# The first mixer's projection begins over half of the features, and the modulation pieces are dealt out differently

## The chip, the cores and the metric

One core of one Trainium2 chip runs the whole program as a single launch. A core has five engines that each take their instructions strictly in the order in which they were queued: TensorE (PE, with its weight load PEld), VectorE (DVE), ScalarE (ACT), GpSimd (POOL) and SyncE (SP, which here only issues DMA transfers). The metric is the device time of one execution in microseconds (us), as the median of several.

## The reference, cut to what matters

Two layers of a transformer-like trunk over 512 latent tokens and 256 context tokens, 1024 features, fp32. The change touches the first mixer of layer 0 alone:

```python
mod_l = silu(c) @ mod_w[l] + mod_b[l]            # 6 x 1024 values: shift, scale, gate, twice
h = x * (1 + scale) + shift                      # the same for the context with c_ctx
z = h @ w_in                                     # 1024 -> 1536 features: 512 pool, 512 a, 512 gate
u = z_a * sigmoid(z_gate)                        # then a depthwise convolution over 31 tokens
y = silu(layer_norm(conv(u)))                    # 4 groups of 128 channels
p = mean over windows of 2, 4, 8, 16 tokens - z_pool, then a 128x128 product per group
out = concat(p, y) @ w_out
```

After it come a residual, a norm and the PEER retrieval, then layer 1 with another mixer. All matrix products of the mixer split each fp32 operand in a high and a low part and add three products.

## The kernel before, in words

**Modulation.** `mod_w` of both layers is cut in 24 pieces of 1024 x 512, 2 MB each; pieces 0 to 11 are layer 0's, and of these 0 and 1 are the first shift (features 0 to 511, and 512 to 1023), 2 and 3 the first scale. `mod_pieces` (L179) loads a piece into one of three buffers `modw`, multiplies it on PE (32 matmuls into `modp`, 64 records in the trace), and copies it on ACT into a row buffer `mrow` (four copies a piece). Its inner function `turned` transposes the row on PE (`modt`, L72 and L198) and adds the bias on DVE (L203, and L205 for a scale). `mods(...)` first turns the group begun before, then begins a new one, so a group is turned one `mods` later. `modp` and `modt` have one buffer each: a group's transposes wait until DVE has read the group before.

**Projection.** Pieces 0, 2, 1, 3 are worked first, then x is loaded in eight blocks of 128 features (`xt`, four buffers), modulated on DVE (L467) and split in `h1h` (ACT) and `h1l` (DVE). The projection then runs in twelve chunks of 128 output features. A chunk is 48 matmuls (8 feature blocks, 3 products, 512 and 256 tokens) into one of three PSUM buffers `zps`; its weights are loaded by SP (`c_raw`, two buffers) and split on ACT (`c_hi`) and DVE (`c_lo`) into three buffers. The first eight chunks come in four pairs (value and gate), then four pool chunks. After a pair, ACT computes the sigmoid `sg` (L545) and DVE the product `upad` (L547, L548).

**Convolution.** Group 0's 31 taps are done as a scaling on ACT (`ctap`, L500, two buffers) and an addition on POOL (`cacc`, L501); groups 1 and 2 as one DVE instruction a tap (L496); group 3 on PE as products with diagonal matrices (`cdh` on ACT L511, `cdl` on DVE L512, six buffers each; six matmuls a tap), which start after the last chunk. `advance(6)` after a chunk queues four taps of each group that runs.

**Pool and end.** `pooled` (L576) forms sums of windows on DVE (`psum`, L584), multiplies and splits them, and a small product on PE follows. The output weights (`wo_raw`, `woh`, `wol`) are split in the same stretch. When all taps are done, a mean over channels is taken on PE with `invn` (L617), and the norm follows.

**What sets the order.** The program is traced in the order written; a list scheduler with a time model of its own then fixes every engine's queue at compile time. At run time the queues are in-order and only semaphores hold an instruction back. After the mean with `invn` the order of PE, DVE and ACT is the same in both kernels to the end of the program, and SP's and POOL's too from before that point on.

Of the kernel before, what the change touches and what calls it, by code (L numbers as in the profile page):

```python
# [9 lines left out]
F32 = mybir.dt.float32  # L10
# [8 lines left out]
P = 128  # L19
D = 1024  # L20
KB = D // P
NLAT, NCTX = 4, 2
NTOK = (NLAT + NCTX) * P
# [52 lines left out]
def kernel(tc, a, out):  # L76
    nc = tc.nc
    V, S, G, PE, SP = nc.vector, nc.scalar, nc.gpsimd, Tracked(nc.tensor), nc.sync
# [7 lines left out]
    def pool(stack, name, bufs=1, space=None, side="left"):  # L86
        return stack.enter_context(tc.tile_pool(name=name, bufs=bufs, space=space, reuse_waits="tile") if space
                                   else tc.tile_pool(name=name, bufs=bufs, side=side, reuse_waits="tile"))
# [9 lines left out]
    def kt(shape, name, dt=F32):  # L98
        return kp.tile(shape, dt, name=name)
# [75 lines left out]
    mrow = [kt([P, P], f"mrow{i}") for i in range(2)]  # L175
# [2 lines left out]

    def mod_pieces(js, room, pp, queue, after=None):  # L179

        ps = pp.tile([P, 2, P], F32, name="modp", bufs=1)
        for i, j in enumerate(js):
            w = room()
            with tc.issue_after(after.ins) if after is not None else nullcontext():
                queue.dma_start(w, a["mod_w"][j // 12, j % 12])
            for k in range(KB):
                for g in range(4):
                    PE.matmul(ps[32 * g:32 * g + 2, i], scT[:, k, :], w[:, k, g * P:(g + 1) * P],
                              start=k == 0, stop=k == KB - 1, tile_position=(0, 32 * g))
        for i, j in enumerate(js):  # L190
            for g in range(4):
                r = slice(32 * g, 32 * g + 2)
                S.copy(mrow[i][r], ps[r, i])

        def turned():
            pt = pp.tile([P, 2, P], F32, name="modt", bufs=1)
            for i, j in enumerate(js):
                PE.transpose(pt[:, i], mrow[i], ident)  # L198
            for i, j in enumerate(js):
                l, j = divmod(j, 12)  # L200
                src = pt[:, i].rearrange("p (g r) -> p g r", r=32)[:, :, :2]
                dst = modT[l][:, 4 * j:4 * j + 4, :]
                V.tensor_tensor(dst, src, mod_bT[:, l, 4 * j:4 * j + 4].unsqueeze(2).to_broadcast([P, 4, 2]), op=OP.add)  # L203
                if j // 2 in (1, 4):
                    V.tensor_scalar_add(dst, dst, 1.0)  # L205

        return turned
# [92 lines left out]
    def split(hi, lo, src):  # L300
        copied[0] = S.copy(hi, src)  # L301
        return V.tensor_tensor(lo, src, hi.bitcast(F32), op=OP.subtract)  # L302

    def spans(n):
        return [(0, 512), (512, 256)] if n == 768 else [(0, n)]

    def mm_chunk(ps, wh, wl, hh, hl, n):

        for k in range(KB):
            for w, h, first, last in ((wh, hh, k == 0, False), (wh, hl, False, False), (wl, hh, False, k == KB - 1)):  # L310
                for o, ln in spans(n):
                    PE.matmul(ps[:, o:o + ln], w[:, k], h[:, k, o:o + ln], start=first, stop=last)
# [120 lines left out]
    def mixer0(gt):  # L433
        with ExitStack() as es:
# [7 lines left out]
            wp = pool(e4, "m0w")  # L442
# [3 lines left out]
            hh = wp.tile([P, KB, NTOK], F32R, name="h1h")  # L446
            hl = wp.tile([P, KB, NTOK], F32R, name="h1l")
            segs = ((0, 0, 512), (527, 512, 256))

            unturned = []  # L450

            def mods(*js):

                while unturned:
                    unturned.pop(0)()
                if js:
                    unturned.append(mod_pieces(js, lambda: mw.tile([P, KB, 512], F32, name="modw", bufs=3), ppS, SP,
                                               loaded[0]))

            for j in (0, 2, 1, 3):  # L460
                mods(j)
            mods()
            for k in range(KB):
                xt = wp.tile([P, NTOK], F32, name="xt", bufs=4)
                SP.dma_start(xt, a["xT"][:, k])
                for s, (o, ln) in enumerate(spans(NTOK)):
                    V.tensor_scalar(xt[:, o:o + ln], xt[:, o:o + ln], modT[0][:, 8 + k, s:s + 1],  # L467
                                    modT[0][:, k, s:s + 1], op0=OP.mult, op1=OP.add)
                split(hh[:, k], hl[:, k], xt)

            def big():
                return ppB.tile([P, NTOK], F32, name="zps", tag="big", bufs=3)

            zorder = [4, 8, 5, 9, 6, 10, 7, 11, 0, 1, 2, 3]
            zparts = []

            def zload():
                if zorder:
                    zparts.append(load_chunk(a["ab_w_in"][zorder.pop(0)], wp, CB, "c", 2))

            def zchunk():

                ps = big()
                mm_chunk(ps, *zparts.pop(0), hh, hl, NTOK)
                zload()
                return ps

            zload()

            def taps(g, up):  # L490

# [31 lines left out]
            def advance(n):  # L523
                with tc.issue_after(anchor[0].ins), tc.issue_after(copied[0].ins):
                    for q, r in running:
                        for _ in range(min(n, r)):
                            next(q, None)
# [10 lines left out]
            for g in range(4):  # L538
                pa = zchunk()
                advance(6)  # L540
                mods(4 + 3 * g)
                pg = zchunk()
                advance(6)
                sg = wp.tile([P, NTOK], F32, name="sg")
                S.activation(sg, pg, AF.Sigmoid)  # L545
                up = ups[g]
                V.tensor_tensor(up[:, 15:527], pa[:, :512], sg[:, :512], op=OP.mult)  # L547
                V.tensor_tensor(up[:, 542:798], pa[:, 512:], sg[:, 512:], op=OP.mult)  # L548
                if g < 3:
                    running.append((taps(g, up), 4))  # L550
                else:
                    uh = cp.tile([P, 813], F32R, name="uph", bufs=1)
                    ul = cp.tile([P, 813], F32R, name="upl", bufs=1)
                    split(uh, ul, up)
                    us.append((g, uh, ul))
                mods(3 * g + 5, 3 * g + 6)
            for g in range(4):
                ps = zchunk()
                zp = gs[g]
                S.copy(zp[:, 8:520], ps[:, :512])  # L560
                S.copy(zp[:, 528:784], ps[:, 512:])
                advance(6)
                mods(16 + 2 * g, 17 + 2 * g)
            mods()
            e4.close()
            ea.close()
# [2 lines left out]
            wp = pool(e5, "m0p")  # L569
# [45 lines left out]
            wp = pool(e5, "m0n")  # L615
# [28 lines left out]
            wp = pool(es, "po")  # L644
            pp = pool(es, "po_ps", 1, PSUM)
# [1064 lines left out]
```

## Time and profile before

| what | value |
|---|---|
| median of 3 runs | 3774.27 us (3770.95 to 3774.3) |
| the profiled execution | 3781.63 us, span 3779.9 us |
| PE busy over the span | 96% |
| DVE busy over the span | 82% |
| first mixer's projection and convolution | first 231 us of the span |

The page of the profile averages over 3780 us and many stages; the change acts on the first 231 us. Read that stretch by itself: first the table of stages, then the order of time on each engine. A row of the order of time gives the start, the length, the engine, the line, what is written from what, how many instructions are merged in the row, and in brackets the idle time before it and what ended that.

### The profile page before, as it was taken

To read this page: it belongs to the slowest core of one execution; us is meant where nothing else is said; L and a number is where in the kernel's file an instruction comes from. 1 tells how busy PE (TensorE), PEld (TensorE's weight loads), DVE (VectorE), ACT (ScalarE), POOL (GpSimd) and SP (SyncE) were. 2 spreads that over 40 slices of the span, in tenths; PEclk is the share of its full clock that TensorE was granted. 3 is DMA by queue.
4 is the path that set the end of the run, shared out by engine and by line. 5 is a ranking of instruction groups with operands and counts; after the bars stand their busy time and mean duration, and the time that the engine had idled before them with its cause. 6 is when DMAs were issued, how large, how long until landed. Compare 5 with 4: busy or idle time off the path is not lost.

```text
span 3779.9 us, 57257 instructions
## 1 busy us (share of the span) xinstructions
PE 3640.1 (96%) x20375; PEld 3165.4 (84%) x20375; DVE 3108.3 (82%) x6574; ACT 1837.1 (49%) x3234; POOL 1707.5 (45%) x1213
## 2 busy tenths in 40 slices
PE   7989999999999999999998999999999999999998
PEld 6768788788888778888887898789999999878876
DVE  4987899999999788888887627589988887778778
ACT  4442322388888732323224435333369998333332
POOL 2400255454455467888871214004412223677773
PEclk9999999999999999999999999899999999999999
DMA  9723588899999989999993110268978989899885
GB/s 372 277 86 130 203 313 326 301 344 361 361 356 362 371 314 347 355 371 361 351 349 124 53 36 1 84 211 298 312 267 310 316 294 349 287 322 334 321 319 198
DMA packets 372830, 1044.01 MB, mean 276 GB/s; under 512 B 31808, under 2 KB 171456, under 8 KB 342080
## 3 DMA queue, kind: packets, MB, share of 16 engines
q1 hardware_dynamic: 260368, 632.14, 45.5%
q0 software_dynamic: 112032, 407.95, 30.2%
q8 instruction: 160, 2.62, 0.3%
q14 instruction: 126, 1.03, 0.1%
q10 hardware_dynamic: 144, 0.26, 0.0%
HBM read 915.98 MB, written 124.26 MB: 275 GB/s over the span
## 4 chain that ended last, share of the span: by engine, by line
PE 67%; DVE 10%; ACT 6%; issue 5%; DMA 5%; POOL 4%; SPq 1%; DVEq 0%; POOLq 0%; ACTq 0%
PE ups L68 32%; PE res L68 18%; PE gps L68 4%; PE tps L68 3%; PE zps L68 2%; POOL w L1088 2%; DMA v_raw<-in_peer_v_dram 2%; PE wops L68 2%; POOL g_row L688 2%; SPq L883 1%; ACT o L837 1%; DMA ag<-A_d 1%; ACT stage L846 1%; DVE cacc L496 1%; PE mlps L68 1%
## 5 line engine op out<-in xcount | busy, mean ns | idle before, releaser
L688 POOL DMA_INDIRECT g_row<-in_peer_u_dram,g_idx x384 | 523.4, 1363 | 821.2 <-DVE g_row L692 319.5
L688 POOL DMA_INDIRECT g_row<-in_peer_v_dram,g_idx x384 | 586.7, 1528 | 299.2 <-DVE g_acc L696 145.9
L301 ACT CAST c_hi<-c_raw 128x1024 fp32r<-128x1024 f32 x304 | 318.7, 1048 | 560.9 <-PE ups L68 494.4
L302 DVE TENSOR_TENSOR v_lo<-v_raw,v_hi 128x1024 fp32r<-128x1024 f32 x256 | 419.9, 1640 | 206.9 <-ACT v_hi L301 206.9
L301 ACT CAST v_hi<-v_raw 128x1024 fp32r<-128x1024 f32 x256 | 269.3, 1052 | 635.7 <-DMA v_raw<-in_peer_v_dram 434.7
L1088 POOL TENSOR_TENSOR w<-ag,gg 128x512 f32<-128x512 f32 (+1 forms) x256 | 445.7, 1741 | 277.4 <-DVE w_lo L302 228.9
L68 PE MATMUL res<-v_hi,w_hi 128*128 128x512 f32 x1792 | 555.8, 391 | 13.0 <-ACT w_hi L301 13.0
L68 PE MATMUL res<-v_lo,w_hi 128*128 128x512 f32 x1792 | 555.4, 390 | 0.5
L68 PE MATMUL res<-v_hi,w_lo 128*128 128x512 f32 x1792 | 554.3, 390 | 0.0
L696 DVE SCALAR_TENSOR_TENSOR g_acc<-g_row,g_act,g_acc 128x1024 f32<-128x1024 f32 x381 | 531.1, 1394 | 2.9
L302 DVE TENSOR_TENSOR c_lo<-c_raw,c_hi 128x1024 fp32r<-128x1024 f32 x304 | 372.4, 1225 | 163.4 <-ACT c_hi L301 160.4
L692 DVE SCALAR_TENSOR_TENSOR g_row<-g_row,g_h 128x1024 f32<-128x1024 f32 x384 | 487.2, 1285 | 4.2 <-DMA g_row<-in_peer_u_dram,g_idx 4.2
L68 PE MATMUL ups<-opah,c_hi 128*128 128x512 f32 x1152 | 458.2, 398 | 3.6 <-ACT c_hi L301 3.6
L68 PE MATMUL ups<-opah,c_lo 128*128 128x512 f32 x1152 | 451.6, 393 | 5.5 <-DVE c_lo L302 5.5
L68 PE MATMUL ups<-opal,c_hi 128*128 128x512 f32 x1152 | 451.9, 392 | 0.0
L68 PEld LDWEIGHTS res<-v_hi,w_hi 128*128 128x128 f32 x1792 | 336.2, 188 | 85.9 <-ACT w_hi L301 16.3
L68 PEld LDWEIGHTS res<-v_lo,w_hi 128*128 128x128 f32 x1792 | 336.2, 188 | 74.5 <-DVE v_lo L302 5.1
L68 PE MATMUL ups<-opch,c_hi 128*128 128x384 f32 x1152 | 393.1, 341 | 4.1 <-ACT c_hi L301 4.1
L68 PEld LDWEIGHTS res<-v_hi,w_lo 128*128 128x128 f32 x1792 | 336.1, 188 | 71.5 <-DVE w_lo L302 2.1
L68 PE MATMUL ups<-opch,c_lo 128*128 128x384 f32 x1152 | 387.9, 337 | 4.1 <-DVE c_lo L302 4.1
L68 PE MATMUL ups<-opcl,c_hi 128*128 128x384 f32 x1152 | 386.6, 336 | 0.0
L837 ACT ACTIVATE o<-iota,ijT 128x128 f32<-128x128 f32 x896 | 292.0, 401 | 0.2
(479 smaller groups left out, 6617.1 us busy)
## 6 DMA issues: line engine op xcount, KB each, us to landing
c_raw<-in_uT_dram SPq DMA_DIRECT2D x256, 512.0 KB, 6.2
v_raw<-in_peer_v_dram SPq DMA_DIRECT2D x128, 1024.0 KB, 7.5
G_d<-stage SPq DMA_DIRECT2D x56, 1024.0 KB, 8.1
modw<-in_mod_w_dram SPq DMA_DIRECT2D x24, 2048.0 KB, 10.6
c_raw<-in_peer_wq_dram SPq DMA_DIRECT2D x64, 512.0 KB, 4.6
gg<-G_d SPq DMA_DIRECT2D x64, 512.0 KB, 10.5
A_d<-at SPq DMA_DIRECT2D x120, 256.0 KB, 5.8
ag<-A_d SPq DMA_DIRECT2D x30, 1024.0 KB, 11.3
```

The costliest lines, as they stand in the source:

```text
L68: self.last = self.engine.matmul(*args, **kw)
L301: copied[0] = S.copy(hi, src)
L302: return V.tensor_tensor(lo, src, hi.bitcast(F32), op=OP.subtract)
L496: V.scalar_tensor_tensor(cacc[:, g], up[:, k:k + 783], conv_w[:, g, k:k + 1], cacc[:, g], op0=OP.mult, op1=OP.add)
L688: G.indirect_dma_start(out=row, out_offset=None, in_=a[f"peer_{'uv'[tab]}{l}"], in_offset=bass.IndirectOffsetOnAxis(ap=idx[i][:, s:s + 1], ...
L692: V.scalar_tensor_tensor(row, row, 1.0, h, op0=OP.mult, op1=OP.mult, accum_out=w)
L696: V.scalar_tensor_tensor(acc, row, w, acc, op0=OP.mult, op1=OP.add)
L837: S.activation(o1[:, i], iota, AF.Abs, bias=tr[:, 0, n0 + i:n0 + i + 1])
L846: S.copy(stg[:, :, b * W8:(b + 1) * W8].rearrange("p i n -> p n i"), pg)
L883: SP.dma_start(vp["gg"][-1][:, r], G_d[:, r, gorder[i]:gorder[i] + GG, :])
L1088: G.tensor_tensor(w.rearrange("p (t m) -> p t m", m=TG), ag[:, i], gg[:, :, (c + i) % GG, :], op=OP.mult)
```

## The change

The projection's start is cut in two. Pieces 0 and 2 are loaded and worked first, then x blocks 0 to 3, and the first three chunks (`begin`) run over feature blocks 0 to 3 only, which fills all three `zps` buffers. Pieces 1 and 3 and x blocks 4 to 7 follow, and `zchunk` finishes the begun chunks over blocks 4 to 7 before it goes on as before. The other twenty pieces are dealt out anew: one after each of the eight paired chunks, and three after each of the four pool chunks (before: one and two in turn, then two). `modp` and `modt` grow to three columns, and a third row buffer is added.

```diff
-        ps = pp.tile([P, 2, P], F32, name="modp", bufs=1)
+        ps = pp.tile([P, 3, P], F32, name="modp", bufs=1)
...
-            pt = pp.tile([P, 2, P], F32, name="modt", bufs=1)
+            pt = pp.tile([P, 3, P], F32, name="modt", bufs=1)
...
-    def mm_chunk(ps, wh, wl, hh, hl, n):
+    def mm_chunk(ps, wh, wl, hh, hl, n, ks=range(KB)):
...
-        for k in range(KB):
+        for k in ks:
...
+            mrow.append(wp.tile([P, P], F32, name="mrow2"))
+            G.memset(mrow[2], 0.0)
...
-            for j in (0, 2, 1, 3):
-                mods(j)
-            mods()
-            for k in range(KB):
+            def xload(k):
...
+            begun = []
+
+            def begin():
+
+                begun.append(big())
+                mm_chunk(begun[-1], *zparts[len(begun) - 1], hh, hl, NTOK, range(KB // 2))
+
             def zchunk():
 
-                ps = big()
-                mm_chunk(ps, *zparts.pop(0), hh, hl, NTOK)
-                zload()
+                if begun:
+                    ps, ks = begun.pop(0), range(KB // 2, KB)
+                else:
+                    ps, ks = big(), range(KB)
+                mm_chunk(ps, *zparts.pop(0), hh, hl, NTOK, ks)
+                if not zparts:
+                    zload()
                 return ps
 
+            mods(0)
+            mods(2)
+            mods()
+            for k in range(KB // 2):
+                xload(k)
             zload()
+            begin()
+            zload()
+            begin()
+            mods(1)
+            mods(3)
+            mods()
+            zload()
+            begin()
+            for k in range(KB // 2, KB):
+                xload(k)
...
-                mods(4 + 3 * g)
+                mods(4 + 2 * g)
...
-                mods(3 * g + 5, 3 * g + 6)
+                mods(5 + 2 * g)
...
-                mods(16 + 2 * g, 17 + 2 * g)
+                mods(12 + 3 * g, 13 + 3 * g, 14 + 3 * g)
```

Three places of the queues show what moves. First, SP's queue at the start of the program, before:

```order
L103 DMA small<-in_smalls_dram 128x300
L185 DMA modw<-in_mod_w_dram 128x4096 x4
L465 DMA xt<-in_xT_dram 128x768 x4
L320 DMA c_raw<-in_ab_w_in_dram 128x1024
L465 DMA xt<-in_xT_dram 128x768 x2
```

and after:

```order
L103 DMA small<-in_smalls_dram 128x300
L185 DMA modw<-in_mod_w_dram 128x4096 x2
L464 DMA xt<-in_xT_dram 128x768 x4
L320 DMA c_raw<-in_ab_w_in_dram 128x1024 x2
L185 DMA modw<-in_mod_w_dram 128x4096 x2
L320 DMA c_raw<-in_ab_w_in_dram 128x1024
L464 DMA xt<-in_xT_dram 128x768 x4
```

Four blocks of x and two chunks' weights stand behind two pieces instead of four.

Second, ACT's queue from the second sigmoid to the third (`ctap` is a tap of group 0, `mrow` a piece's copies), before:

```order
L545 ACTIVATE sg<-zps 128x768
L301 CAST c_hi<-c_raw 128x1024
L193 COPY mrow_79<-modp 2x128 x4
L193 COPY mrow_80<-modp 2x128 x4
L500 ACTIVATE ctap<-upad_333,small 128x783 x4
L301 CAST c_hi<-c_raw 128x1024
L500 ACTIVATE ctap<-upad_333,small 128x783 x3
L193 COPY mrow_79<-modp 2x128 x4
L500 ACTIVATE ctap<-upad_333,small 128x783
L545 ACTIVATE sg<-zps 128x768
```

and after:

```order
L570 ACTIVATE sg<-zps 128x768
L301 CAST c_hi<-c_raw 128x1024
L525 ACTIVATE ctap<-upad_422,small 128x783
L193 COPY mrow_79<-modp 2x128 x4
L525 ACTIVATE ctap<-upad_422,small 128x783 x3
L301 CAST c_hi<-c_raw 128x1024
L525 ACTIVATE ctap<-upad_422,small 128x783 x4
L193 COPY mrow_79<-modp 2x128 x4
L301 CAST c_hi<-c_raw 128x1024
L525 ACTIVATE ctap<-upad_422,small 128x783 x4
L570 ACTIVATE sg<-zps 128x768
```

Twelve taps stand between the two sigmoids instead of eight, and the first of them is no longer behind a group of two pieces.

Third, DVE's queue from its last convolution taps to the first pool sum (`modT` is a turned piece), before:

```order
L496 SCALAR_TENSOR_TENSOR cacc<-upad_335,small,cacc 128x783 x9
L584 TENSOR_TENSOR psum<-g_acc 128x791
L203 TENSOR_TENSOR modT_78<-modt,small 128x8 x2
L205 TENSOR_SCALAR modT_78<-modT_78 128x8 x2
L302 TENSOR_TENSOR pwl<-pw,pwh 128x512
L587 TENSOR_TENSOR psum<-psum,pinv 128x776
```

and after:

```order
L521 SCALAR_TENSOR_TENSOR cacc<-upad_424,small,cacc 128x783 x7
L203 TENSOR_TENSOR modT_78<-modt,small 128x8 x2
L205 TENSOR_SCALAR modT_78<-modT_78 128x8
L203 TENSOR_TENSOR modT_78<-modt,small 128x8 x4
L205 TENSOR_SCALAR modT_78<-modT_78 128x8
L537 SCALAR_TENSOR_TENSOR cdl<-ident,small,cdh 128x128 x11
L203 TENSOR_TENSOR modT_78<-modt,small 128x8 x2
L205 TENSOR_SCALAR modT_78<-modT_78 128x8
L203 TENSOR_TENSOR modT_78<-modt,small 128x8
L609 TENSOR_TENSOR psum<-g_acc 128x791
```

The first pool sum stands behind the additions of the last nine pieces and eleven `cdl`. On PE the transposes of pieces 21 to 23 stand, after the last chunk, behind three transposes, 65 to 71 of group 3's tap matmuls and the pieces' own products; before, the last chunk was followed by two transposes, 13 tap matmuls, and the products and transposes of pieces 22 and 23.

## Rows read from the trace of the kernel before

**Rows 1.** Table by stage: window, length, busy us of each engine (instructions), PEclk, DMA, GB/s

```profile
0.00:33.00 33.00, 12.31 (x261) 8.52 (x261) 10.46 (x27) 10.99 (x29) 1.79 (x32) 0.91 0.87 344
...
104.00:130.00 26.00, 20.08 (x194) 16.98 (x183) 26.00 (x18) 12.42 (x22) 21.12 (x9) 0.99 0.68 263
130.00:150.00 20.00, 19.99 (x312) 16.07 (x313) 20.00 (x17) 9.09 (x18) 9.38 (x4) 0.85 0.67 256
...
188.10:231.30 43.20, 38.35 (x231) 31.84 (x219) 42.13 (x78) 24.43 (x55) 0.00 (x0) 1.00 0.33 108
```

**Rows 2.** Order of time, the start: pieces, x, and the first chunk

```profile
9.08 3.59 PE L68 MATMUL modp<-modw,scT 128*2 128x128 f32 x64 [9.08 <-DMA modw<-in_mod_w_dram]
...
14.22 1.93 PE L68 MATMUL modp<-modw,scT 128*2 128x128 f32 x64
...
17.43 0.33 PE L72 MATMUL modt<-ident,mrow 128*128 128x128 f32 x1 [1.27 <-ACT mrow L193]
20.00 3.56 PE L68 MATMUL modp<-modw,scT 128*2 128x128 f32 x64 [2.25 <-DMA modw<-in_mod_w_dram]
25.82 1.77 DVE L467 TENSOR_SCALAR xt<-xt,modT 128x512 f32<-128x512 f32 x4 [0.47 <-DMA xt<-in_xT_dram]
27.59 0.96 DVE L302 TENSOR_TENSOR h1l<-xt,h1h 128x768 fp32r<-128x768 f32 x1
32.85 1.01 PE L68 MATMUL zps<-h1h,c_hi 128*128 128x512 f32 x2 [3.79 <-ACT c_hi L301]
```

**Rows 3.** Order of time, PE: end of the third chunk, a piece, the fourth chunk

```profile
66.72 0.38 PE L72 MATMUL modt<-ident,mrow 128*128 128x128 f32 x2
67.03 1.93 PE L68 MATMUL modp<-modw,scT 128*2 128x128 f32 x64
68.89 0.62 PE L68 MATMUL zps<-h1h,c_hi 128*128 128x512 f32 x2
...
77.48 0.27 PE L72 MATMUL modt<-ident,mrow 128*128 128x128 f32 x1
```

**Rows 4.** Order of time, POOL from 60 to 190 us: group 0's thirty taps

```profile
64.38 16.61 POOL L501 TENSOR_TENSOR cacc<-cacc,ctap 128x783 f32<-128x783 f32 x8 [61.94 <-ACT ctap L500]
86.06 22.00 POOL L501 TENSOR_TENSOR cacc<-cacc,ctap 128x783 f32<-128x783 f32 x9 [5.08 <-ACT ctap L500]
...
140.32 14.76 POOL L501 TENSOR_TENSOR cacc<-cacc,ctap 128x783 f32<-128x783 f32 x6 [14.47 <-ACT ctap L500]
```

**Rows 5.** Order of time, DVE from 78 to 190 us

```profile
78.91 0.69 DVE L547 TENSOR_TENSOR upad<-zps,sg 128x512 f32<-128x512 f32 x1 [0.95 <-ACT sg L545]
...
113.81 13.82 DVE L496 SCALAR_TENSOR_TENSOR cacc<-upad,small,cacc 128x783 f32<-128x783 f32 x6
...
129.63 0.23 DVE L203 TENSOR_TENSOR modT<-modt,small 128x8 f32<-128x8 f32 x2
129.78 7.64 DVE L496 SCALAR_TENSOR_TENSOR cacc<-upad,small,cacc 128x783 f32<-128x783 f32 x8
...
175.76 12.43 DVE L496 SCALAR_TENSOR_TENSOR cacc<-upad,small,cacc 128x783 f32<-128x783 f32 x12
188.11 0.97 DVE L584 TENSOR_TENSOR psum<-g_acc 128x791 f32<-128x791 f32 x1
```

**Rows 6.** Order of time, PE at two later places

```profile
130.01 0.44 PE L72 MATMUL modt<-ident,mrow 128*128 128x128 f32 x1 [5.92 <-DVE modT L203]
130.38 6.46 PE L68 MATMUL modp<-modw,scT 128*2 128x128 f32 x128
...
183.48 0.38 PE L72 MATMUL modt<-ident,mrow 128*128 128x128 f32 x2
...
231.34 4.97 PE L68 MATMUL zps<-cacc,invn 128*128 128x512 f32 x14 [0.42 <-DVE invn L617]
```

**Rows 7.** Groups by shape, DVE from 188.05 to 236.7 us: busy us, mean ns, idle before

```profile
L302 DVE TENSOR_TENSOR wol<-wo_raw,woh 128x1024 fp32r<-128x1024 f32 x8 | 9.8, 1220 | 3.2 <-ACT woh L301 3.2
L512 DVE SCALAR_TENSOR_TENSOR cdl<-ident,small,cdh 128x128 fp32r<-128x128 f32 x25 | 7.7, 344 | 0.7 <-ACT cdh L511 0.7
```

## The prediction

> **What bounds the kernel now.** The change touches only the first 231 us; from the channel mean with `invn` on, the queues are the same, so whatever moves that mean moves the end. I read the table by stage first [rows 1], to see which engine is full where: PE is short of work up to 33 us (12.31 busy of 33), DVE is full from 104 to 150 us while PE is not, and from 188.1 to the mean DVE is again busy for 42.13 of 43.20 us. Then I read the order of time, engine by engine.
>
> The start waits for data: four pieces of 2 MB stand ahead of x on SP's queue, x arrives at 25.82, and the first chunk starts at 32.85 [rows 2]. From there to about 104 us PE runs through: a chunk takes 8.59 us (68.89 to 77.48), a piece 1.93 [rows 3]. Then DVE takes over. Its tap costs 0.955 us alone (7.64 over 8) and 2.30 while POOL adds its own taps (13.82 over 6) [rows 5]; a POOL tap takes 2.08 us alone (16.61 over 8) and 2.44 to 2.46 beside DVE (22.00 over 9, 14.76 over 6) [rows 4]. In such a stretch one DVE instruction with two operands in SBUF gets through per POOL tap. So DVE falls behind its queue, and PE, whose transpose needs the addition of the group before, stands 5.92 us until 130.01; the two pieces behind that wait take 6.46 us instead of 3.86 [rows 6], at a mean granted clock of 0.85 of the 2.4 GHz level from 130 to 150 us [rows 1]. From 130 on PE runs through again: the last chunk ends at 183.48 [rows 6]. DVE's last convolution tap ends at 188.1 and the pool sums follow at once [rows 5]; 43.2 us later the mean starts, at 231.34, released by DVE's `invn` [rows 6].
>
> **The start.** Two pieces and then x: piece 2 is multiplied at 14.22 and turned by 17.8 as before [rows 2]. Piece 1, the third in line before, arrived at 20.00; four x blocks and one chunk's weights are 2.1 MB, as much as that piece, so they arrive by about 20. A block costs DVE 0.95 and 0.96 us [rows 2], so four cost 7.6, and with a chunk's `c_lo` (1.22, as a `wol` of the same shape [rows 7]) half chunks flow from about 25 instead of 33. But PE then needs pieces 1 and 3 (3.9 us and two waits of 1.3 for the copies), the second scale is turned at about 42, and DVE needs another 7.6 us for blocks 4 to 7: the three second halves cannot end their first chunk before about 50. With pieces 4 and 5 and 12.7 us of second halves, three chunks are done at about 63. Before it was 66.7, with one piece more (1.93). So of 8 us at the start 2 are left at this point. Pieces 1 and 3 land some 7 us later, behind x, at about 27 and 32; PE asks for them at 34 and 38, so that costs nothing.
>
> **The middle.** POOL's first tap before, at 64.38, followed the copies of two pieces [rows 4]; now one piece's, at about 61.8. Eight lone taps end at 78.4, and they hold ACT, so the second sigmoid moves only from 78 to 75 or 76. Then group 1 begins on DVE. ACT's queue now holds 12 taps of group 0 up to the third sigmoid and 8 to the fourth: 20 POOL taps, nearly without a pause (before: a pause of 5 us, then 16). DVE has some 25 two-operand instructions from its second product to the addition of piece 9, for which PE's transpose after the eighth chunk waits. Twenty of them pair with a POOL tap: 20 x 2.44 = 48.8; five are alone, 4.8; a product, 1.1. That is 78.4 + 54.7 = 133. The same counting for the kernel before gives 134 where the trace has 129.6, since its small instructions wait less; I take 130, no change. PE by itself would be there at 63 + 5 x 8.59 + 5 x 1.93 = 116. So the bounds are 116 and 134 against 130.0: -14 to +4, and I take 0, because the row for the same wait is nearest.
>
> **From there to the last chunk** PE runs through in both. Before, 8 pieces and 4 chunks stand in this stretch (53.5 us, from 130.01 to 183.48 [rows 6]); now 10 pieces, as fewer were dealt out earlier: 2 x 1.93 = **+3.9**. Last chunk at 187.4.
>
> **The tail.** This is the largest term. Before, DVE goes from its last tap to the pool sums at 188.1, which is 4.6 us after the last chunk. Now the additions of pieces 18 to 23 stand ahead of the first pool sum on DVE's queue, and PE brings the last of them late: after the last chunk it has 71 tap matmuls (a chunk's 48 in 8.59 us is 0.179 each [rows 3]: 12.7 us), three pieces (5.8), six transposes of 0.2 (1.2), and it waits for the row copies twice (1.1 to 1.3 each, as in [rows 2]). That is 22 us, in which DVE has only eleven `cdl` of 0.34 us to do [rows 7]. The pool sums start at 187.4 + 22 instead of 183.5 + 4.6: **+17.4** on top of the +3.9. If the copies and the transposes hid wholly it would be 18 instead of 22; if the pieces came late from memory, more.
>
> **What the tail gives back.** Behind that point DVE has 11 `cdl` fewer (3.8 us) and fewer additions (0.7), but `invn` now stands behind all eight `wol` instead of six (2 x 1.22): **-2.1**. That counts in full, because DVE fills that stretch [rows 1].
>
> Sum: 0 + 3.9 + 17.4 - 2.1 = +19 us. The profiled execution would go from 3781.63 (span 3779.9) to about 3801. It lies 7.4 us above the median of the runs, 3774.27, and I add the difference to the median: **3793 us**.
>
> The Trainium skill, SBUF — State Buffer, section "Who interferes with whom", speaks against this change: a VectorE instruction with two SBUF inputs and a GpSimd instruction that reads SBUF lock each other out for the whole instruction. The trace agrees in kind (2.30 against 0.955 us), so a POOL tap begun earlier on a busy DVE buys nothing. By this rule the middle would come out as in the last rival; the sum goes by the rows.
>
> **The rivals.**
> *DVE is not in the way in the middle.* PE runs at its own pace to 116 (-14), and only the tail costs: -14 + 3.9 + 17.4 - 2.1 = +5, about 3779. For it: POOL's taps start earlier and some fall where DVE has nothing to do. Against: 20 taps in a row beside DVE, where the row has 2.30 us for one.
> *PE sets the end, not DVE.* If the stretch after the last chunk hung on PE, the taps done during the wait would be gain: last chunk at 174, then 186 tap matmuls (33.3), 3 pieces, 24 pool matmuls (4.2) and the turns, 47 in all: 221 instead of 231.3, about 3764. It decides once DVE needs under 25 us behind the last addition. Against: 42.13 busy of 43.20 [rows 1].
> *The start does not come early*, because x or the weights are not there by 20 us, or because halves and pieces wait on each other. The first chunks then come 3 to 6 us later than I think, POOL and DVE with them: 3797 to 3800.
> *Three pieces a turn are bound by DMA.* A turn of the last four brings 6.5 MB in 14.9 us, 440 GB/s; the start had 344 [rows 1]. At 360 GB/s a turn takes 18.1 us: 4 x 3.2 = +13, about 3806. Against: three buffers are filled ahead, and a late PE leaves time.
> *POOL and DVE exclude each other strictly.* A pair of taps then costs 2.08 + 0.955 = 3.04 us, and the 20 pairs of the middle 61 instead of 49: 12 us later, about 3805. Against: the rows have 2.44 for a pair [rows 4].
>
> **How the numbers follow.** Forecast 0.45 (its own range 3785 to 3802), DVE not in the way 0.18, PE sets the end 0.06, late start 0.13, DMA 0.12, strict exclusion 0.06. The range of 8 in 10 leaves out the PE case and the low part of the second, and the top of the DMA and lock cases: 3776 to 3805. About 0.2% (7.5 us) is what a measurement of this kernel can tell from no change: slower by more has 0.45 + 0.13 + 0.12 + 0.06 = 0.76, within it 0.18, faster 0.06.
>
> **What would show it.** In the profile after, the first chunk's matmuls should start at 22 to 25 us with gaps, and three chunks be done near 63. The third sigmoid should not come before 101. PE should stand twice for a `modT` addition between 100 and 135, and its granted clock drop there. The last chunk should end at 182 to 192. DVE should be idle for most of 20 us ahead of the first pool sum, released by PE's `modt`, and that sum should start at 203 to 214. If the sum starts before 190, or if PE never waits for `modT`, the forecast is wrong; if it starts late and the mean still comes by 231, then DVE did not set that stretch.

## The result, and the profile after

The changed kernel takes 3801.20 us (median of 4 runs, 3798.95 to 3803.98) against 3773.89 us (4 runs, 3770.95 to 3774.3): ratio 1.0069, 95% interval 1.0058 to 1.0081, so 27 us slower. Its profiled execution took 3802.78 us (span 3801.0).

Where the time goes is read from three rows of order of time: the end of the last chunk, the start of the pool sums, the start of the mean. The fence takes the changed kernel's engines and SP's queue together.

```profile
61.09 60.21 POOL L526 TENSOR_TENSOR cacc<-cacc,ctap 128x783 f32<-128x783 f32 x25 [58.50 <-ACT ctap L525]
...
62.33 0.17 DVE L203 TENSOR_TENSOR modT<-modt,small 128x8 f32<-128x8 f32 x1 [2.92 <-PE modt L72]
...
78.70 2.25 DVE L517 TENSOR_SCALAR cacc<-upad,small 128x783 f32<-128x783 f32 x1
80.99 10.25 DVE L521 SCALAR_TENSOR_TENSOR cacc<-upad,small,cacc 128x783 f32<-128x783 f32 x4
...
104.48 0.81 ACT L570 ACTIVATE sg<-zps 128x768 f32<-128x768 f32 x1
...
115.58 0.15 DVE L203 TENSOR_TENSOR modT<-modt,small 128x8 f32<-128x8 f32 x1
115.88 0.45 PE L72 MATMUL modt<-ident,mrow 128*128 128x128 f32 x1 [9.93 <-ACT c_hi L301]
...
133.72 0.15 DVE L203 TENSOR_TENSOR modT<-modt,small 128x8 f32<-128x8 f32 x1
134.02 0.45 PE L72 MATMUL modt<-ident,mrow 128*128 128x128 f32 x1 [4.76 <-DVE modT L203]
134.40 3.59 PE L68 MATMUL modp<-modw,scT 128*2 128x128 f32 x64
...
149.73 40.11 SPq L185 DMA_DIRECT2D modw<-in_mod_w_dram  x9
...
191.24 0.27 PE L72 MATMUL modt<-ident,mrow 128*128 128x128 f32 x1
...
193.33 0.31 DVE L203 TENSOR_TENSOR modT<-modt,small 128x8 f32<-128x8 f32 x3 [10.14 <-PE modt L72]
...
207.55 1.93 PE L68 MATMUL modp<-modw,scT 128*2 128x128 f32 x64
...
209.90 0.35 DVE L537 SCALAR_TENSOR_TENSOR cdl<-ident,small,cdh 128x128 fp32r<-128x128 f32 x1 [2.75 <-PE zps L68]
213.24 0.35 DVE L537 SCALAR_TENSOR_TENSOR cdl<-ident,small,cdh 128x128 fp32r<-128x128 f32 x1 [2.98 <-ACT cdh L536]
213.51 0.23 DVE L203 TENSOR_TENSOR modT<-modt,small 128x8 f32<-128x8 f32 x2
...
213.78 0.16 DVE L203 TENSOR_TENSOR modT<-modt,small 128x8 f32<-128x8 f32 x1
213.86 0.97 DVE L609 TENSOR_TENSOR psum<-g_acc 128x791 f32<-128x791 f32 x1
...
216.66 0.96 DVE L612 TENSOR_TENSOR psum<-psum,pinv 128x776 f32<-128x776 f32 x1
...
257.23 4.97 PE L68 MATMUL zps<-cacc,invn 128*128 128x512 f32 x14 [0.60 <-DVE invn L642]
```

GpSimd's taps now run from 61 to 121 us with hardly a pause (25 in 60.21 us; [rows 4] had gaps), and DVE's taps beside them take 2.56 us each (10.25 over 4) from their first. PE's transpose stands twice, until 115.88 and 134.02. The row at 115.88 names ACT's `c_hi`, which a transpose doesn't read; DVE's addition of 115.58 ended at 115.73, 0.15 us before the transpose, the same distance as at 134.02. The piece behind each wait takes 3.6 instead of 1.93 us. The last chunk ends at 191.4 (183.6 before, [rows 6]). Behind it PE does the last three pieces, the third at 207.55, between tap matmuls; DVE waits for them, `cdl` by `cdl` and then with the additions at 213.51 and 213.78, and the pool sums start 22.5 us after the last chunk (4.5 before, [rows 5]). The mean starts at 257.23 instead of 231.34: **+25.9 us, as much as the times lose**. The two profiled executions differ by less, 21.2 us: the one of before was 7.7 us above its median, and behind the mean, where the queues are the same, it took 4.8 us longer than the changed kernel's.

The tables by stage for the same kernel (columns as in [rows 1]):

```profile
67.00:100.00 33.00, 31.82 (x340) 26.96 (x339) 25.46 (x15) 19.70 (x30) 31.98 (x14) 1.00 0.57 222
100.00:134.00 34.00, 19.33 (x147) 15.35 (x146) 33.86 (x22) 14.82 (x22) 28.56 (x12) 0.77 0.44 173
...
184.00:192.00 8.00, 7.67 (x98) 6.24 (x96) 0.00 (x0) 2.24 (x9) 0.00 (x0) 1.00 1.03 403
...
191.20:213.90 22.70, 21.36 (x277) 16.94 (x276) 4.67 (x20) 10.22 (x33) 0.00 (x0) 1.00 0.47 175
213.90:257.20 43.30, 29.21 (x135) 23.67 (x133) 41.36 (x63) 20.82 (x39) 0.00 (x0) 0.76 0.30 104
```

From 100 to 134 DVE is full and PE has work for 19.33 of 34 us, at a granted clock of 0.77. From 191.2 to 213.9 DVE has work for 4.67 of 22.7 us: that is the wait of the tail. From 67 to 134 the DMA engines are half idle (0.57, 0.44), and full at 184 to 192 (1.03), where the postponed pieces come (nine issued from 149.73 on, within 40.11 us).

### The profile page after: what moved, and what is told of

Same layout as the page of the kernel before. It is cut to its first block, busy times and chain, and to the rows that moved or that the text cites. A ratio compares the mean times of both kernels' runs of the same rounds, so it can differ in the third digit from the quotient of the medians.

```text
span 3801.0 us, 57258 instructions
## 1 busy us (share of the span) xinstructions
PE 3641.7 (96%) x20375; PEld 3165.2 (83%) x20375; DVE 3099.1 (82%) x6574; ACT 1838.2 (48%) x3234; POOL 1708.8 (45%) x1214
## 3 DMA queue, kind: packets, MB, share of 16 engines
q14 instruction: 126, 1.03, 0.1%
## 4 chain that ended last, share of the span: by engine, by line
PE 69%; DVE 10%; ACT 6%; issue 5%; DMA 4%; POOL 4%; SPq 1%; DVEq 0%; POOLq 0%; ACTq 0%
PE ups L68 31%; PE res L68 21%; PE gps L68 4%; PE tps L68 3%; PE zps L68 2%; POOL w L1113 2%; DMA v_raw<-in_peer_v_dram 2%; PE wops L68 2%; POOL g_row L713 1%; ACT o L862 1%; ACT stage L871 1%; DVE cacc L521 1%; PE mlps L68 1%; DMA ag<-A_d 1%; PE modp L68 1%
## 5 line engine op out<-in xcount | busy, mean ns | idle before, releaser
L713 POOL DMA_INDIRECT g_row<-in_peer_v_dram,g_idx x384 | 573.2, 1493 | 299.1 <-DVE g_acc L721 148.8
L1113 POOL TENSOR_TENSOR w<-ag,gg 128x512 f32<-128x512 f32 (+1 forms) x256 | 458.3, 1790 | 276.5 <-DVE w_lo L302 228.3
L302 DVE TENSOR_TENSOR v_lo<-v_raw,v_hi 128x1024 fp32r<-128x1024 f32 x256 | 405.2, 1583 | 216.7 <-ACT v_hi L301 216.3
```

The costliest lines, as they stand in the source:

```text
L713: G.indirect_dma_start(out=row, out_offset=None, in_=a[f"peer_{'uv'[tab]}{l}"], in_offset=bass.IndirectOffsetOnAxis(ap=idx[i][:, s:s + 1], ...
L1113: G.tensor_tensor(w.rearrange("p (t m) -> p t m", m=TG), ag[:, i], gg[:, :, (c + i) % GG, :], op=OP.mult)
```

## The experiments

Four numbers describe each run: the end of the last chunk; the delay from there to the second step of the first pool group (`psum` times `pinv`, the first step that needs all the queues); from there to the mean; and the time over the kernel before, from the ratio of runs on the same chip, with its 95% interval. All profile numbers are of one execution; starts of executions differ by some 2 us, and what a run adds at the mean and in its time differ by up to 6 us (after_no0: +5.4 and 0).

| kernel | last chunk ends | to second step | to mean | mean at | us over before |
|---|---|---|---|---|---|
| before | 183.6 | 6.3 | 41.4 | 231.3 | 0 |
| changed | 191.4 | 25.3 | 40.6 | 257.2 | +26 (22 to 31) |
| start_alone | 190.0 | 10.1 | 41.6 | 241.6 | +10 (6 to 14) |
| deal_alone | 196.5 | 25.3 | 40.7 | 262.5 | +31 (25 to 37) |
| late_turn | 191.8 | 17.6 | 40.5 | 249.9 | +19 (13 to 25) |
| pool_first_only | 191.3 | 15.3 | 42.6 | 249.2 | +20 (15 to 26) |
| pool_first | 191.4 | 9.9 | 44.9 | 246.1 | +18 (12 to 23) |
| pace3 | 195.5 | 25.3 | 40.8 | 261.5 | +25 (19 to 31) |
| after_no0 | 170.6 | 25.3 | 40.8 | 236.7 | 0 (-4 to +3) |
| before_no0 | 175.6 | 5.2 | 42.9 | 223.7 | -12 (-16 to -7) |
| start_pool_first | 188.6 | 6.5 | 42.5 | 237.6 | +5 (1 to 8) |
| before_pool_first | 185.5 | 6.0 | 44.0 | 235.6 | +3 (-2 to +7) |
| start_pace | 186.9 | 13.4 | 40.7 | 241.1 | +6 (3 to 10) |
| swap | 177.5 | 4.6 | 53.8 | 235.9 | +3 (0 to 6) |

The theory: the dealing makes the loss, through pieces done later and through work paced by the last pieces that stands ahead of the pool sums. Rivals: the half start itself costs; PE's own work sets the end.

**start_alone and deal_alone: the two halves of the change.** start_alone is the changed kernel with

```diff
-                mods(4 + 2 * g)
+                mods(4 + 3 * g)
-                mods(5 + 2 * g)
+                mods(3 * g + 5, 3 * g + 6)
-                mods(12 + 3 * g, 13 + 3 * g, 14 + 3 * g)
+                mods(16 + 2 * g, 17 + 2 * g)
```

and deal_alone is the kernel before with these lines the other way round (and room for three pieces).

> The half start alone, with the pieces dealt as before (one, then two, in the turns of the first eight chunks, two in each of the last four). Theory A, that the dealing makes the loss (last chunk 8 us later, then the pool sums 18 us later behind the additions of the last pieces on DVE's queue): the pool sums start 4 to 8 us after the last chunk again, the first mean matmul starts near 231 (225 to 237, as against 257 in the changed kernel and 231 before), and the time is 3768 to 3780, within 0.2% of before. Rival B, that the half start costs by itself (its taps come earlier in a bunch, the transposes of the middle wait on DVE): last chunk's end 188 or later, mean at 238 or later, time 3782 or more. Rival C, that start and dealing are each harmless and only hurt together, says the same as A here and differs in the next kernel.

> The new dealing alone (one piece fewer in each turn of the first eight chunks' pairs, three in each of the last four, modulation tiles for three), with the start of before: all eight chunks over all features, nothing begun early. Theory A: the last chunk ends near 190 (187 to 196), the pool sums start about 22 us after it (18 to 26), the mean starts at 252 to 262, and the time is 3790 to 3802, +16 to +28 over before. Rival B (the half start costs): time 3770 to 3780, mean at 229 to 236. Rival C (only together): the same as B here. Were three pieces a turn held up by their loads, matmuls modp would stand for DMA modw for over 10 us between 140 and 200.

Measured: 3785.1 us and 3807.44 us against 3776.87. The dealing alone costs all of it and more; its tail is that of the changed kernel to the tenth (25.3 us). So the theory holds for the dealing, though deal_alone lies a little beyond its ranges (last chunk 196.5 for 187 to 196, +31 for +16 to +28). But the half start alone costs 10 us, where the theory had 3780 at most and rival B was right. DVE's first tap of group 1, and the wait of PE after the eighth chunk with the addition that ends it, in start_alone and then in deal_alone:

```profile
86.23 2.22 DVE L517 TENSOR_SCALAR cacc<-upad,small 128x783 f32<-128x783 f32 x1
...
133.52 0.15 DVE L203 TENSOR_TENSOR modT<-modt,small 128x8 f32<-128x8 f32 x1
133.82 0.45 PE L72 MATMUL modt<-ident,mrow 128*128 128x128 f32 x1 [9.77 <-DVE modT L203]
```

```profile
83.92 1.38 DVE L494 TENSOR_SCALAR cacc<-upad,small 128x783 f32<-128x783 f32 x1
...
137.76 0.15 DVE L203 TENSOR_TENSOR modT<-modt,small 128x8 f32<-128x8 f32 x1
138.06 0.45 PE L72 MATMUL modt<-ident,mrow 128*128 128x128 f32 x1 [8.51 <-DVE modT L203]
```

Both wait longer for DVE than the kernel before (5.92, [rows 6]). The two costs don't add up to 26: under the new dealing the half start brings the last chunk 5 us earlier (196.5 to 191.4), under the old one 6 us later. The traces show where the sign changes. All times here are counted from the first sigmoid, so that the differing starts of executions drop out:

| kernel | to DVE's first tap of group 1 | from there to the addition that PE waits for | two-operand taps in it |
|---|---|---|---|
| before | 27.7 | 47.6 | 16 |
| start_alone | 29.3 | 47.3 | 16 |
| deal_alone | 28.6 | 53.8 | 20 |
| changed | 22.9 | 55.0 | 19 |

The longer second stretch comes with the dealing, which puts three or four taps more ahead of that addition. The first stretch is where the two edits don't add up: ahead of the second sigmoid on ACT's queue stand eight taps of group 0 behind the copies of two pieces under the old dealing, eight behind one piece's in the changed kernel, and twelve in deal_alone. So the half start gains there only together with the new dealing. Why the scheduler puts four taps more there in deal_alone stays open.

**late_turn, pool_first_only, pool_first: what holds the pool sums.** late_turn moves the last turn behind the pooled groups; pool_first_only puts each pooled group before its six diagonal taps; pool_first does both (where the turn moves, the third row buffer also goes to a pool that stays open for it):

```diff
             for g in range(4):
+                pooled(g)
                 for _ in range(6):
                     next(rest)
                     advance(1)
-                pooled(g)
+            mods()
             e5.close()
```

> The changed kernel with one edit: the last turn (transposes and additions of pieces 21 to 23) stands behind the four pooled groups in the program, so that the first pool sum is no longer behind their additions on DVE's queue. Theory A, that the 18 us of the tail are that place in the queue: the first pool sum starts 2 to 10 us after the last chunk (22.6 in the changed kernel), the mean starts at 238 to 248 (257.2), and the time is 3783 to 3793, 8 to 18 us under the changed kernel. Rival D, that PE's own order (three pieces and 71 tap matmuls after the last chunk) sets the end whatever DVE does: the pool sums start early but the mean stays within 3 us of 257 and the time within 3797 to 3805.

> The changed kernel with one edit of the tail: each pooled group before its six diagonal taps; the last turn stays where it is, ahead of them. The additions of pieces 21 to 23 still stand ahead of the first pool sum on DVE, but TensorE has no tap matmuls to put between these pieces. Theory A2: the three pieces (5.8 us) and six transposes with their copies follow the last chunk at once, the first sum starts 7 to 12 us after the last chunk (22.6 in the changed kernel), the mean at 240 to 249, the time 9 to 18 us over before. Rival D: mean at 252 or later, time 21 us or more over before.

> The changed kernel with the order of the tail rewritten in two places: each pooled group comes before its six diagonal taps instead of behind them, and the last turn (pieces 21 to 23) comes behind all of it. So neither the additions of the last pieces nor the diagonals cdl, which wait for TensorE's tap matmuls, stand ahead of the pool sums on DVE's queue. Theory A2 (the tail is lost because work paced by TensorE stands ahead of the pool sums in DVE's queue, additions and diagonals alike): first sum at 191 to 193, second step (times pinv) at 193 to 198 (209.4 in late_turn, 216.7 in the changed kernel), mean at 235 to 242 and the time 4 to 12 us over before. Rival D (TensorE's own work after the last chunk sets the mean): mean at 247 or later, time 18 us or more over before.

DVE in late_turn:

```profile
191.93 0.98 DVE L608 TENSOR_TENSOR psum<-g_acc 128x791 f32<-128x791 f32 x1 [8.17 <-PE zps L68]
193.75 0.31 DVE L203 TENSOR_TENSOR modT<-modt,small 128x8 f32<-128x8 f32 x3 [0.83 <-PE modt L72]
...
204.04 0.35 DVE L537 SCALAR_TENSOR_TENSOR cdl<-ident,small,cdh 128x128 fp32r<-128x128 f32 x1 [2.74 <-PE zps L68]
...
209.40 0.96 DVE L611 TENSOR_TENSOR psum<-psum,pinv 128x776 f32<-128x776 f32 x1
```

The first sum starts 0.1 us after the last chunk (2 to 10 expected), and the second step not before 209.4: nine `cdl` stand between them, each waiting for a `cdh` whose buffer PE's tap matmuls free. A queue that is cleared of one late instruction stops at the next. Mean 249.9 and time 3796.82, above theory A's 238 to 248 and 3783 to 3793, but short of rival D's mean of 254 or later. In pool_first_only DVE has no `cdl` there and waits for the additions alone:

```profile
193.56 0.17 DVE L205 TENSOR_SCALAR modT<-modT 128x8 f32<-128x8 f32 x1
204.78 0.24 DVE L203 TENSOR_TENSOR modT<-modt,small 128x8 f32<-128x8 f32 x2 [11.05 <-PE modt L72]
...
205.13 0.97 DVE L609 TENSOR_TENSOR psum<-g_acc 128x791 f32<-128x791 f32 x1
```

The first sum comes 13.9 us after the last chunk (7 to 12 expected), the mean at 249.2 (240 to 249; rival D 252 or later), +20 us (9 to 18; rival D 21 or more): between the two. With both gone, pool_first, DVE waits for the load of `pw`, through ACT. The last rows are the end of the stretch behind the second step, and its row of the table by stage (columns as in [rows 1]):

```profile
191.38 0.33 SPq L595 DMA_DIRECT2D pw<-in_pool_w_dram  x1
...
198.45 1.93 PE L68 MATMUL modp<-modw,scT 128*2 128x128 f32 x64 [1.60 <-DMA modw<-in_mod_w_dram]
...
199.96 0.62 ACT L301 CAST pwh<-pw 128x512 fp32r<-128x512 f32 x1 [6.21 <-DMA pw<-in_pool_w_dram]
...
200.61 0.69 DVE L302 TENSOR_TENSOR pwl<-pw,pwh 128x512 fp32r<-128x512 f32 x1 [6.81 <-ACT pwh L301]
201.22 0.96 DVE L611 TENSOR_TENSOR psum<-psum,pinv 128x776 f32<-128x776 f32 x1
...
243.64 0.17 DVE L642 MEMSET invn<- 128x128 f32 x1
...
246.12 5.33 PE L68 MATMUL zps<-cacc,invn 128*128 128x512 f32 x16
...
201.20:246.10 44.90, 41.41 (x213) 35.05 (x214) 38.60 (x72) 23.27 (x56) 0.00 (x0) 0.92 0.25 79
```

`pw`, 256 KB, is issued at 191.38, as the last chunk ends, and used at 199.96: the last postponed piece was issued 1.9 us before it and is still on its way, and PE itself waits 1.60 us for that piece. So the delay has three layers: additions and diagonals on DVE's queue (25.3 to 9.9), and under them the loads. Of the 19.0 us by which the changed kernel's delay exceeds that of before, the two edits take 15.4; 4.3 of it are given back behind the second step, where the diagonals are now late: 186 tap matmuls stand there instead of 94, PE is busy for 41.41 of 44.90 us, and the mean follows 2.3 us after `invn` is done, with PE at work in between. There PE sets the mean, as rival D had it. So neither theory came out whole: mean 246.1 (235 to 242, or 247 or later), time +18 (4 to 12, or 18 or more).

**start_pool_first and before_pool_first: the same tail with two late pieces.**

> The half start with the old dealing, and the tail rewritten as in pool_first (each pooled group before its six diagonal taps, the last turn behind all of it). Theory A2 (DVE, and behind it ScalarE, must not hold work paced by the last pieces ahead of the pool sums): step two of the first pool group at 193 to 198 (200.0 in start_alone), mean at 234 to 240 (241.6), the time 3 to 8 us over before (9.8 in start_alone). Rival H (with only two late pieces their loads and matmuls are no longer what the sums wait for, and DVE's own pool work sets the stretch): mean at 240 to 244, time 8 to 12 us over before.

> The kernel before with the same rewriting of its tail, as a control. In before DVE ends its taps at 188.1 and only one diagonal stands ahead of the first pool group, so theory A2 gives nothing to gain: first sum at 187 to 189, second step at 189 to 191, mean at 229 to 234, time within 4 us of before. Rival I (the order pooled-first is worth some 8 us in any kernel, so that the runs with it say nothing about the late pieces): mean at 220 to 226, time 5 us or more under before.

Measured: 3782.49 and 3782.6 against 3777.93. With the old dealing the second step comes 6.5 us after the last chunk, as in the kernel before, in which the rewriting gains nothing (+3, interval -2 to +7; mean 235.6, above its 229 to 234). It takes 15.4 us off the delay of the changed kernel, 3.6 off start_alone's and 0.3 off before's, so what pool_first won belongs to pieces that are late. With this tail the half start costs 2 us at the mean (237.6 for 235.6) and nothing that the times can tell, so a good part of start_alone's 10 us lies in the tail too.

**after_no0 and before_no0: the middle without GpSimd.**

```diff
-                for k in range(1, CONV_W):
+                for k in range(1, CONV_W if g else 2):
```

> The changed kernel without taps 2 to 30 of the first convolution group, so without nearly all of the additions on GpSimd and their multiplications on ScalarE (the output is that of a shorter filter in one group). Theory F (the middle is set by VectorE's taps that take 2.5 us beside GpSimd's and 1.0 us alone, and by ScalarE's queue behind GpSimd): no DVE tap over 1.3 us, third sigmoid before 95 (104.5), TensorE waits under 3 us for modT between 90 and 140, last chunk ends at 168 to 180 (191.4), the mean at 233 to 246, time 11 to 24 us under the changed kernel. Rival E (DVE's own taps and the loads set the middle): third sigmoid at 100 or later, last chunk at 185 or later, time within 6 us of the changed kernel.

> The kernel before, with the same taps left out, as the partner of the run without them in the changed kernel. Theory F: its smaller wait in the middle goes too, last chunk at 172 to 179 (183.6), mean at 219 to 227 (231.3), time 4 to 12 us under before; the difference to its changed partner falls from 27 to 13 to 24 us, since the part of the change's loss that is made in the middle is gone and the part in the tail is not. Rival E: time within 3 us of before and a difference to the partner of 24 to 30.

DVE in after_no0:

```profile
77.82 4.25 DVE L521 SCALAR_TENSOR_TENSOR cacc<-upad,small,cacc 128x783 f32<-128x783 f32 x4
...
172.56 0.31 DVE L203 TENSOR_TENSOR modT<-modt,small 128x8 f32<-128x8 f32 x3 [16.03 <-PE modt L72]
...
193.09 0.97 DVE L609 TENSOR_TENSOR psum<-g_acc 128x791 f32<-128x791 f32 x1
```

The four taps that took 10.25 us take 4.25, PE waits nowhere between 60 and 170, and the last chunk ends 20.8 us earlier, 8.0 in before. Now the changed kernel reaches the end of the last chunk 5 us before its partner, one piece of 1.93 included. With GpSimd's taps it is 7.8 us behind: 12.8 us of the change are lost in the middle to group 0's taps. The run takes away GpSimd's additions and ScalarE's scalings together, so it does not tell what the pairs cost from what ACT's queue costs. The tail is untouched: 25.3 us again, though everything before it moved by 21. The difference between the partners falls to 11 us (3773.8 and 3763.24 against 3775.43), just under the 13 to 24 expected, and to 13.0 at the mean; after_no0 is 26 to 27 us under the changed kernel (11 to 24 expected). The Trainium skill (SBUF — State Buffer, "Who interferes with whom") has such pairs shut each other out; the trace agrees in kind, with 2.56 us for a pair, less than the 3.04 of the prediction's strict rival.

**pace3 and start_pace: fewer GpSimd taps ahead of the third sigmoid.**

```diff
-                    running.append((taps(g, up), 4))
+                    running.append((taps(g, up), 4 if g else 3))
```

> The changed kernel with one edit: the taps of group 0 (ScalarE and GpSimd) are handed out three a step instead of four, so that fewer of them lie beside DVE's taps before the third sigmoid. Theory A holds the crowd of 20 such taps for the cause of the 4 us that the middle loses (the transpose after the eighth chunk at 134.0 instead of 130.0): that transpose goes back to 128 to 131, the mean starts 3 to 6 us earlier than 257.2, the pool sums still start about 22 us after the last chunk, and the time is 3794 to 3800. Rival E, that DVE's taps take as long whatever GpSimd does: transpose at 133 to 135, time 3799 to 3804.

> The half start with the old dealing, and group 0's taps three a step. In pace3 this took the wait from the third sigmoid (96.0 instead of 104.5) and put one of 8 us behind the nine taps left over, which stand on ScalarE's queue ahead of the copies of the pieces. Theory F (DVE and GpSimd share what the middle can do, so a wait that goes in one place comes back in another): third sigmoid at 95 to 99, last chunk not before 186 (190.0 in start_alone), mean at 236 to 244, time 4 to 12 us over before. Rival J (with the old dealing fewer copies stand behind the leftover taps, so the early start is kept): last chunk at 178 to 184, mean at 228 to 234, time from 6 under to 1 over before.

In pace3 the third sigmoid came at 96.0, PE's first wait for `modT` fell to 5.5 us and its second, after the eighth chunk, to 0.3 (at 125.5), and then this, on ACT and PE:

```profile
159.33 0.95 ACT L525 ACTIVATE ctap<-upad,small 128x783 f32<-128x783 f32 x1 [1.58 <-POOL cacc L526]
160.18 3.33 ACT L193 COPY mrow<-modp 2x128 f32<-2x128 f32 x12
...
161.32 0.48 PE L72 MATMUL modt<-ident,mrow 128*128 128x128 f32 x1 [7.98 <-ACT mrow L193]
```

The nine taps left over stand on ACT's queue ahead of the pieces' copies and go at GpSimd's pace; the wait moved to a later place and grew. Last chunk 195.5, time unchanged: my numbers were wrong, though the crowd of taps did hold the third sigmoid. In start_pace the last chunk and the time were as theory F had them (186.9; 3786.12, no gain on start_alone, their intervals overlap), the third sigmoid was not (102.0 for 95 to 99). The 3 us won at the last chunk go in the delay behind it, 13.4 instead of 10.1.

**swap: DVE takes the first two groups.**

```diff
-                    if g in (1, 2):
+                    if g in (0, 1):
```

> start_pool_first with one edit: the convolution groups change engines, VectorE takes the first two (ready at the first and second sigmoid) and ScalarE with GpSimd the third; before it was the second and third on VectorE and the first on GpSimd. VectorE is nearly idle up to 79 in all kernels run and nearly always busy from 100 to 188, so this starts its taps 20 us earlier, and the first of them run without GpSimd beside them. Theory F (the middle is bound by VectorE's taps and their slow pairs with GpSimd's, which is why an earlier start of the chunks bought nothing): third sigmoid at 92 to 98 (102.9 in start_pool_first), no wait of TensorE for modT over 3 us between 60 and 185, last chunk at 174 to 182 (188.4), mean at 221 to 230 (237.6), time 2 to 12 us under before. Rival K (GpSimd's 30 taps now begin near 100, stand on ScalarE's queue ahead of the copies of the pieces and hold TensorE as in pace3): last chunk at 184 or later, mean at 234 or later, time from 1 to 12 us over before.

The middle did mostly as theory F said: no wait for `modT`, last chunk at 177.5, though the third sigmoid came at 101.6 (92 to 98 expected). But GpSimd's group now comes last. POOL and DVE in swap:

```profile
182.13 0.96 DVE L611 TENSOR_TENSOR psum<-psum,pinv 128x776 f32<-128x776 f32 x1
...
192.72 13.44 POOL L526 TENSOR_TENSOR cacc<-cacc,ctap 128x783 f32<-128x783 f32 x6 [11.83 <-ACT ctap L525]
...
204.66 1.65 DVE L537 SCALAR_TENSOR_TENSOR cdl<-ident,small,cdh 128x128 fp32r<-128x128 f32 x1
```

Six taps fall among the pool sums, where a `cdl` takes 1.65 instead of 0.34 us, and the stretch from the second step to the mean grows from 42 to 54 us, DVE's busy time in it from 38.6 to 47.8. The 11 us won are lost there; mean 235.9 and 3777.29 against 3774.75 (+3) are rival K's numbers, though not by its path: PE was not held, GpSimd's late taps slowed the pool sums. No version that does all the work beat the kernel before.

## Why the prediction was right, and where its sizes were off

Direction and mechanism were right; the size, +19 us, fell short of +26 to +27. By its own terms, from the rows:

- Start: three chunks done by 62.3 (the addition behind them; 63 predicted), third sigmoid at 104.48 (not before 101 predicted). Right.
- Middle: 0 predicted, +4.0 measured (134.02 for 130.01). This is the term that was mis-sized: I had worked out 133 from 20 pairs of 2.44 us and taken 130, because the same counting gave 134 for before where the trace had 129.6. The value worked out was the better one; correcting it by another kernel's error was the mistake. DVE's first tap of group 1 came at 78.70 (78.4 in the working) and the addition 55.0 us later (54.7). That this fits so well is partly luck: a pair took 2.56 us, and 15 taps paired. The rows had that price already. Of DVE's six taps in 13.82 us [rows 5] the last ran alone, since POOL's taps beside them ended at 125.86, so five pairs took 2.56 each; the 2.30 and 2.44 of the prediction are means over pairs and lone taps:

```profile
108.25 17.61 POOL L501 TENSOR_TENSOR cacc<-cacc,ctap 128x783 f32<-128x783 f32 x7 [0.18 <-ACT ctap L500]
```

- To the last chunk: +3.9 predicted, +3.8 measured.
- Tail: the first sum was to start 22 us after the last chunk instead of 4.6; it was 22.5 instead of 4.5, so +18.0 for +17.4. The size was right, the cause only half: the prediction named the additions of the last pieces and took the eleven `cdl` for harmless filler. late_turn and pool_first showed that the diagonals hold the queue as well, and the postponed loads under both.
- Give-back: -2.1 predicted, +0.1 measured (43.4 us for 43.2 from first sum to mean). DVE's busy time fell by only 0.8 us (41.36 for 42.13, [rows 1]), and its idle time, short waits for ACT and PE, rose from 1.1 to 1.9.
- Of the rivals, "DVE is not in the way" is what after_no0 shows when GpSimd's taps are gone. The start did come early: first matmuls at 21.8, three chunks by 62.3. "Bound by DMA" was not the first limit (PE waited for no piece after the start) but the next one under it. Strict exclusion asked for 12 us in the middle at 3.04 a pair; 4.0 came, at 2.56. "PE sets the end" is refuted for the changed kernel: the mean waits for DVE's `invn`, with PE busy for 29.21 of the 43.30 us, and the taps done during the wait won nothing. It is not refuted beyond it: in the five runs with a rewritten tail, and in swap, the mean follows 1.8 to 2.3 us after `invn` with PE at work.

## What to carry to other kernels

Before work is started earlier, look at who is full in the stretch that follows: here GpSimd's taps came beside VectorE's sooner, and the gain of 5 us at the third chunk had turned into a loss of 4 after the eighth; two more pieces behind it made it 8. Before work is put off, read each in-order queue behind the point at which it now ends: every instruction that waits for it, directly or through a buffer, holds whatever stands behind it, and clearing one only shows the next. A wait that is removed should be followed to the next fixed point (here the last chunk, the second pool step, the mean) before it is booked as a gain.

## What was not expected of the hardware

- Beside GpSimd's taps not only VectorE's two-operand taps are slow: the one with a scalar and a single tensor took 2.25 us (at 78.70) and 0.68 alone, a `cdl` of 128x128 1.65 instead of 0.34, a `c_lo` 2.90 (at 91.16) instead of 1.22, and a one-tensor instruction of 128x8 1.81 (at 117.18) instead of 0.17. The loss in these is 1.3 to 1.7 us, however short the instruction. Those that read an operand from PSUM were not slowed: the product `upad` took 0.68 us at 114.65 beside a GpSimd tap and 0.69 alone.
- GpSimd took 2.08 us for a tap in the eight ahead of VectorE's [rows 4], in which one ran beside a `c_lo` and took 2.87 (1.96 each without it), and 2.56 beside VectorE in these 10.25 us, so that in a pair VectorE loses 1.6 us and GpSimd 0.6.
- A load of 256 KB landed 2.8 us after its issue in the kernel before and 8.4 in the changed one, where a piece of 2 MB had been issued 1.9 us ahead of it and landed 0.6 us before it. In the kernel before, the last piece had landed 2.5 us before the issue.
